# Sums of weights written over the raw chunk in a streaming fp32 encoder trunk

## The chip, the core and the metric

The kernel runs on one core of one Trainium2 chip. Its engines are named as in the profile: PE (TensorE, with PEld for its weight loads), DVE (VectorE), ACT (ScalarE), POOL (GpSimd) and SP (SyncE, which here only issues transfers). Each engine works through its own queue in order, and semaphores hold an instruction until what it needs is there. The metric is the time of one execution on the device, in microseconds; lower is better.

## What is computed

Two layers of an encoder over 256 positions of width 2048, all in float32. The first layer mixes positions with a gated MLP, the second with latent attention; each mixer is followed by a gated MLP with a short convolution:

```python
z = gelu(x @ w_in); u, v = split(z)             # 2048 -> 2 x 6144
s = einsum(w_s * mask, layer_norm(v)) + b_s
x = layer_norm(ALPHA * x + (u * s) @ w_out)     # 6144 -> 2048
h = causal_conv3(x @ w_up) + conv_b             # 2048 -> 2 x 5504
a, g = split(h)
x = layer_norm(ALPHA * x + (silu(g) * a) @ w_down)   # 5504 -> 2048
# second layer: low-rank q/kv projections, 16 heads, rotary part, masked softmax,
# output projection, then the same conv MLP
```

Weights are read once from memory (some 540 MB), so the kernel streams them in chunks of 1 MB.

## The kernel before

**Precision by splitting.** PE multiplies in a rounded fp32 form. Each operand is split into a rounded part and a remainder: ACT casts (`wh`, line 119 or 127), DVE subtracts (`wl`, line 120 or 128). A product is then three matmuls: high by high, low by high, high by low.

**Chunks and pairs.** `Feed` (line 72) loads chunks in a fixed order, splits them and hands them out. `next()` (line 197) hands out the next one and, before that, sees to it that a number of later chunks are split (`splits`) and loaded (`loads`). In the stages v (the second half of the first projection), wo (`w_out`) and dn (`w_down`) a chunk is a pair of 128-row blocks of weights against a pair of blocks of activations, 128x2048 values in four blocks of 512 columns. Such a pair is of one of three kinds:

- wide (`eight`, line 408): eight block products, 24 matmuls.
- seven (`seven`, line 415): Strassen's scheme in Winograd's form, seven block products, 21 matmuls. It needs four sums of the weight blocks (`_seven`, line 130) and of the activations. The sums of weights are made by DVE from the raw chunk (line 134), then split like the weights themselves into `th` and `tl`. The partial results are put together at the end of a group by `rest` (line 425): ACT copies one bank, DVE does four additions; these wait for the last seven products of the group.
- parked: a seven pair whose splitting is done long ahead, in the u and up stages, by `park` (line 146). The four parts go to memory through POOL's queue and are fetched again by `_fetch` (line 179) when the pair comes up for loading.

The v stage has six groups of eight pairs; group 0 is all wide, groups 1 to 5 hold four wide and four seven pairs each (order: wide, seven, wide, seven, wide, seven, seven, wide). wo goes twice over 24 pairs (7 seven pairs each time), each dn stage twice over 21 pairs and a half (10 seven and 8 parked in all). That makes 54 seven pairs and 16 parked ones. The other stages (u, up, the attention's projections, mo) have none.

**Buffers.** On-chip tiles of chunk size come from two sets: "big" with 17 places, "side" with 6. A place comes free when the last instruction that reads its tile is done, and whoever takes it next waits for that: a load waits on SP's queue, a fetch on POOL's. A seven pair takes `raw`, the sums `ts`, `wh`, `wl`, `th` and `tl`.

**What sets the order.** A scheduler places the instructions of each engine when the program is built, by priority and its own estimate of times. `behind` (line 227) adds ordering edges by which a transfer is placed not ahead of the matmul issued last in program order; it adds no wait. With them, the loads of the first chunks stand behind the nine warm-up matmuls (lines 269 and 270) in that order.

In `_seven`, DVE makes the sums into a tile of its own, in three operations (the first makes two sums at once), and the cast of the sums is made in two pieces:

```python
add(two(t, 0), two(raw, 512), raw[:, None, 0:512].to_broadcast([P, 2, 512]))
add(t[:, 1024:1536], t[:, 0:512], raw[:, 1024:1536])
self._cast(wh[:, 0:1536], wl[:, 0:1536], raw[:, 512:2048])
add(t[:, 1536:2048], t[:, 1024:1536], raw[:, 1536:2048])
for c in (slice(0, 1536), slice(1536, 2048)):
    self._cast(th[:, c], tl[:, c], t[:, c])
```

Of the kernel before, what the change touches and what calls it, by code (L numbers as in the profile page):

```python
# [8 lines left out]
F32 = mybir.dt.float32  # L9
F32R = mybir.dt.float32r  # L10
BF16 = mybir.dt.bfloat16
AF = mybir.ActivationFunctionType
ALU = mybir.AluOpType
AX = mybir.AxisListType

P = 128
# [44 lines left out]
        NF_FF: ("0e 1e 2s 3e 4p 5s 6e 7e 8s 9e 10e 11p 12s 13e 14e 15s 16e 17s 18p 19e 20e 21e",  # L61
                "21e 20p 19e 18p 17s 16e 15p 14s 13e 12e 11p 10s 9e 8e 7p 6s 5e 4e 3e 2e 1e 0e")}
KINDS = {"e": "wide", "s": "seven", "p": "parked"}
KEEP = {"wide": 5, "seven": 9, "parked": 6}


# [5 lines left out]
class Feed:  # L72
# [10 lines left out]
    def _load(self):  # L83
        ap, cols, kind = self.chunks[self.loaded][:3]
        if kind == "parked":
            self.parts[self.loaded] = self._fetch(self.loaded)
            self.loaded += 1
            return
        t = self.pool.tile([P, 2048], F32, tag="big", name=f"raw{self.loaded}", bufs=SLOTS["big"])
        step = 512 if self.loaded == 0 else cols  # L90
        if len(ap.shape) == 3:
            self.behind(self.nc.sync.dma_start(t.rearrange("p (k c) -> p k c", k=ap.shape[1]), ap))
        else:
            if self.loaded in (1, 2):
                step = 1024
            for o in range(0, cols, step):
                self.behind(self.nc.sync.dma_start(t[:, o : o + step], ap[:, o : o + step]))
                if self.loaded == 0 and o == step:
                    self.between[0]()
        self.raw[self.loaded] = t  # L100
        self.loaded += 1
# [28 lines left out]
    def _seven(self, i, raw):  # L130

        add = lambda o, a, b: self.nc.vector.tensor_tensor(o, a, b, ALU.add)  # L134
        tile = lambda name, dt: self.pool.tile([P, 2048], dt, tag="big", name=f"{name}{i}", bufs=SLOTS["big"])
        t, wh, wl, th, tl = tile("ts", F32), tile("wh", F32R), tile("wl", F32R), tile("th", F32R), tile("tl", F32R)
        two = lambda a, o: a[:, o : o + 1024].rearrange("p (n c) -> p n c", n=2)
        add(two(t, 0), two(raw, 512), raw[:, None, 0:512].to_broadcast([P, 2, 512]))
        add(t[:, 1024:1536], t[:, 0:512], raw[:, 1024:1536])
        self._cast(wh[:, 0:1536], wl[:, 0:1536], raw[:, 512:2048])  # L140
        add(t[:, 1536:2048], t[:, 1024:1536], raw[:, 1536:2048])
        for c in (slice(0, 1536), slice(1536, 2048)):
            self._cast(th[:, c], tl[:, c], t[:, c])
        return wh, wl, th, tl

    def park(self, i):

        nc, pin = self.nc, self.pin
        tile = lambda n, dt: self.pool.tile([P, 2048], dt, tag="side", name=f"{n}{i}", bufs=SLOTS["side"])
        add = lambda o, a, b: pin(nc.vector.tensor_tensor(o, a, b, ALU.add))  # L150
        two = lambda a, o: a[:, o : o + 1024].rearrange("p (n c) -> p n c", n=2)
        self.kept[i] = kept = {}

        def store(n, t, cols):
            d = self.dram.tile([P, cols], F32, tag=f"kept{n}{i}", name=f"kept{n}{i}", bufs=1)
            pin(nc.gpsimd.dma_start(d, t[:, 0:cols].bitcast(F32)))
            kept[n] = d

        ap = self.chunks[i][0]
        raw = tile("praw", F32)  # L160
        pin(nc.gpsimd.dma_start(raw.rearrange("p (k c) -> p k c", k=ap.shape[1]), ap))
        yield
        yield
        yield
        t = tile("pts", F32)
        add(two(t, 0), two(raw, 512), raw[:, None, 0:512].to_broadcast([P, 2, 512]))
        add(t[:, 1024:1536], t[:, 0:512], raw[:, 1024:1536])
        add(t[:, 1536:2048], t[:, 1024:1536], raw[:, 1536:2048])
        yield
        for n, src, o, cols in (("w", raw, 512, 1536), ("t", t, 0, 2048)):  # L170
            hi, lo = tile(f"p{n}h", F32R), tile(f"p{n}l", F32R)
            pin(nc.scalar.copy(hi[:, 0:cols], src[:, o : o + cols]))
            pin(nc.vector.tensor_tensor(lo[:, 0:cols], src[:, o : o + cols], hi[:, 0:cols].bitcast(F32), ALU.subtract))
            store(f"{n}h", hi, cols)
            store(f"{n}l", lo, cols)
            if n == "w":
                yield

    def _fetch(self, i):

        got = []
        for n in ("wh", "wl", "th", "tl"):
            d = self.kept[i].pop(n)
            t = self.pool.tile([P, 2048], F32R, tag="side", name=f"f{n}{i}", bufs=SLOTS["side"])
            self.behind(self.nc.gpsimd.dma_start(t[:, 0 : d.shape[1]], d))
            got.append(t)
        return got

    def ahead(self, n_load, n_split):
        while self.split < min(n_split, len(self.chunks)):  # L190
# [6 lines left out]
    def next(self, splits=2, loads=2):  # L197
        i = self.used
        self.ahead(i + 1 + splits + loads, i + 1 + splits)
        self.used += 1  # L200
        return self.parts.pop(i)


@with_exitstack
def trunk(ctx: ExitStack, tc: tile.TileContext, x, xT, gm_in, gm_wout, ffn_up, ffn_dn,
          ml_q, ml_kv, ml_b, ml_out, consts, w_sT, b_s, ropes, ln_rows, out):
    nc = tc.nc
# [8 lines left out]
    recent = [None]  # L216
# [9 lines left out]

    def behind(ins):

        if recent[0] is not None:
            tc.add_manual_dep(ins.ins, recent[0].ins.name, mybir.DependencyInfo(mybir.DependencyClass.NoSync,  # L230
                                                                       mybir.DependencyReason.DATA), reason="pace")


    chunks, parked = [], []
# [57 lines left out]
    for j in range(4):  # L292
        t = slot([P, 4, S], f"xraw{j}")
# [103 lines left out]
    class Banks:  # L397
# [17 lines left out]
        def seven(self, a, sums, wh, wl, th, tl):  # L415
            s1, s2, s3, s4 = sums
            self.to("q3", s4, wh, wl, 512)
            self.to("p2", a[0][1], wh, wl, 1024)
            self.to("p1", a[0][0], wh, wl, 0)
            self.to("q4", a[1][1], th, tl, 1536)  # L420
            self.to("q5", s1, th, tl, 0)
            self.to("p7", s3, th, tl, 512)
            self.to("p6", s2, th, tl, 1024)

        def rest(self):
# [150 lines left out]
    class Norm:  # L576
# [11 lines left out]
        def fetch(self, h):  # L588

            if h in self.res:  # L590
                return
            t = slot([P, 2, 1024], f"res{self.idx}_{h}")
            for b in range(2):
                src = x[b * P : (b + 1) * P, h * 1024 : (h + 1) * 1024] if self.away is None else self.away[h][:, b, :]
                nc.sync.dma_start(t[:, b, :], src)
            self.res[h] = t
# [98 lines left out]
    for gi in range(6):  # L695

        acc = Banks(f"v{gi}", DIRECT if gi == 0 else DIRECT + OWN if gi % 2 else OWN + DIRECT)
        rest = (None,) * 4
        for c, p in enumerate(V_PAIRS[gi]):
            a = [[x_parts(xhl, 2 * p + j, b) for j in range(2)] for b in range(2)]  # L700
            got = feed.next()
            if p in V_SEVEN[gi]:
                acc.seven(a, xc[p], *got)
                if p == V_SEVEN[gi][-1]:
                    rest = acc.rest()
            else:
                acc.eight(a, *got)
            if gi == 0 and p in V_SEVEN[1]:
                x4 = xraw[p // 2]
                room = xc_room[len(xc) // 2][:, len(xc) % 2, :]  # L710
                xc[p] = combine(p, room, x4[:, 2 * (p % 2)], x4[:, 2 * (p % 2) + 1])
            if c == 2 and gi > 0:
                stats(gi - 1)
        vt = slot([P, 2, 1024], f"v{gi}", tag="side")
        for i, (n, t) in enumerate(zip(DIRECT, rest)):
            o = vt[:, i // 2, (i % 2) * 512 : (i % 2) * 512 + 512]
            if t is not None:
                nc.vector.tensor_tensor(o, acc.acc[n], t, ALU.add)
            nc.scalar.activation(o, acc.acc[n] if t is None else o, AF.Gelu_apprx_tanh,
                                 accum_out=vsum[:, i // 2, 2 * gi + i % 2 : 2 * gi + i % 2 + 1])  # L720
        v.append(vt)
        if gi == 0:
            nc.sync.dma_start(cst, consts)
            nc.sync.dma_start(rope_sb, ropes)

            lnrow = tp.tile([P, P], F32, tag="t1", name="lnrow", bufs=T1)
            nc.sync.dma_start(lnrow, ln_rows.rearrange("r (k p) -> (r k) p", p=P))
        if gi == 4:

            wT = slot([P, 2, 1024], "wT")  # L730
            wTg = wT[:, 0, :].rearrange("p (g i) -> p g i", g=NG)
            nc.sync.dma_start(wTg, w_sT)
            nc.gpsimd.memset(wTg[64:P, :, 0:64], 0.0)
            bsum = slot([P, 2, 1024], "bsum")
            nc.sync.dma_start(bsum[:, 1, :], b_s.to_broadcast([P, 1024]))
# [517 lines left out]
```

## Time and profile before

| | |
|---|---|
| median of 3 runs | 2503.91 us (2501.18 to 2511.24) |
| the profiled execution | 2503.74 us, span 2501.9 us |
| busy share of the span: PE, PEld, DVE, ACT | 99%, 85%, 79%, 57% |
| memory read and written | 539 MB and 65 MB, 241 GB/s over the span |
| stages by time (us from the span's start) | v to about 262, u to 560, wo to 815, up to 1288, dn to 1520, attention and mo to 1860, second up to 2264, second dn to 2502 |

A row of busy time by stage gives the stretch and its length, then for PE, PEld, DVE, ACT and POOL the busy time with the number of instructions in brackets, then the granted clock of PE as a share of full speed, the busy share of the DMA engines and GB/s. A row of the timeline gives start, duration, engine, line, operation, output and inputs with their shapes, and in square brackets the engine's idle time just before and what ended it. A row of waits gives who waited for whom, the total in us, how often, and the longest. A row of the chain of waits gives start, length and the work; a row of groups the busy time, the mean of one in ns, and the idle time before. Matmuls overlap in the records: their rate is read from the starts.

### The profile page before, as it was taken

The page shows a single profiled execution, that of the slowest core. Times are in us where ns is not written, and L with a number is a line of the kernel's source. Part 1 is how long each engine was busy: PE and PEld are TensorE (multiplying, and loading weights), DVE is VectorE, ACT ScalarE, POOL GpSimd, SP SyncE. Part 2 cuts the span into 40 slices and gives each one's busy share as a digit, 9 for nine tenths or more (in the row PEclk, how much of TensorE's full clock was granted, in tenths as well). Part 3 has the DMA queues.
Part 4 walks back from the last instruction along what each step waited for, and adds up shares of the span by engine and source line. Part 5 has one row for each costly group of instructions (what it writes and reads, how often), then busy time and mean ns, then how long its engine had stood idle before and what let it go on. Part 6 is the DMA issues. An engine that isn't in the chain of part 4 may idle for free.

```text
span 2501.9 us, 33396 instructions
## 1 busy us (share of the span) xinstructions
PE 2472.1 (99%) x12995; PEld 2123.2 (85%) x12995; DVE 1987.7 (79%) x2779; ACT 1425.2 (57%) x1976; POOL 84.8 (3%) x165
## 2 busy tenths in 40 slices
PE   9999999999999999999999999999999999999998
PEld 7887888888888888888887878988888888887886
DVE  6999866679898798796678878856698787768887
ACT  5666644456565666565555456564566665555543
POOL 0000000000000010000000100000000000000010
PEclk9999999999999999999999999999999999999999
DMA  6555644556566689787547984543589789556795
GB/s 245 201 217 203 218 170 169 185 178 216 201 201 214 247 337 356 293 331 277 185 168 286 341 323 165 181 168 129 189 315 352 277 340 361 200 173 231 278 375 196
DMA packets 109503, 606.17 MB, mean 242 GB/s; under 512 B 10272, under 2 KB 11040, under 8 KB 62112
## 3 DMA queue, kind: packets, MB, share of 16 engines
q1 hardware_dynamic: 85984, 465.61, 52.0%
q0 software_dynamic: 23360, 138.42, 14.1%
q8 instruction: 102, 1.67, 0.2%
q14 instruction: 57, 0.47, 0.1%
HBM read 538.98 MB, written 65.01 MB: 241 GB/s over the span
## 4 chain that ended last, share of the span: by engine, by line
PE 87%; DVE 5%; DMA 4%; issue 2%; ACT 1%; SPq 0%; POOL 0%; DVEq 0%; ACTq 0%; POOLq 0%
PE up L225 35%; PE u L225 11%; PE wo_q L225 5%; PE v_q L225 4%; PE dn_q L225 4%; PE mo L225 4%; PE v_p L225 4%; PE wo_p L225 3%; PE dn_p L225 3%; DMA raw<-in_ffn_dn_dram 3%; PE wo_e L225 2%; PE upf L225 2%; PE v_e L225 1%; DVE wl L120 1%; PE dn_e L225 1%
## 5 line engine op out<-in xcount | busy, mean ns | idle before, releaser
L120 DVE TENSOR_TENSOR wl<-raw,wh 128x1024 fp32r<-128x1024 f32 (+3 forms) x640 | 877.9, 1392 | 241.4 <-ACT wh L119 211.4
L119 ACT CAST wh<-raw 128x1024 fp32r<-128x1024 f32 (+3 forms) x640 | 743.4, 1189 | 336.2 <-DVE wl L120 71.2
L225 PE MATMUL up<-xhl,wh 128*128 128x512 f32 x2624 | 611.1, 390 | 0.0
L225 PEld LDWEIGHTS up<-xhl,wh 128*128 128x128 f32 x2624 | 487.4, 188 | 97.7
L225 PEld LDWEIGHTS up<-xhl,wl 128*128 128x128 f32 x2624 | 325.8, 192 | 6.4
L225 PE MATMUL up<-xhl,wl 128*128 128x256 f32 x2624 | 328.1, 283 | 0.0
L225 PE MATMUL u<-xhl,wh 128*128 128x512 f32 x768 | 182.5, 392 | 0.2 <-DVE h_u L380 0.2
L225 PEld LDWEIGHTS u<-xhl,wh 128*128 128x128 f32 x768 | 141.7, 188 | 29.0 <-DVE h_u L380 0.7
L127 ACT CAST th<-ts 128x1536 fp32r<-128x1536 f32 x106 | 111.2, 1052 | 86.4 <-DVE ts L134 76.0
L128 DVE TENSOR_TENSOR tl<-ts,th 128x1536 fp32r<-128x1536 f32 x106 | 126.4, 1219 | 0.6 <-ACT th L127 0.2
L225 PEld LDWEIGHTS u<-xhl,wl 128*128 128x128 f32 x768 | 95.6, 191 | 3.1 <-DVE wl L120 1.0
L127 ACT CAST wh<-raw 128x1536 fp32r<-128x1536 f32 x53 | 78.5, 1481 | 33.6 <-DVE wl L120 8.3
L225 PE MATMUL u<-xhl,wl 128*128 128x256 f32 x768 | 96.6, 283 | 0.8 <-DVE wl L120 0.8
L128 DVE TENSOR_TENSOR wl<-raw,wh 128x1536 fp32r<-128x1536 f32 x53 | 92.9, 1752 | 0.5 <-PE wo_p L225 0.4
L225 PE MATMUL mo<-wh,oT 128*128 128x512 f32 x256 | 82.6, 403 | 0.0
L134 DVE TENSOR_TENSOR ts<-raw 128x1024 f32<-128x1024 f32 x53 | 64.7, 1220 | 17.4 <-DMA raw<-in_ffn_dn_dram 10.4
L225 PE MATMUL v_q<-wh,xhl 128*128 128x512 f32 x224 | 70.2, 395 | 4.6 <-ACT wh L119 4.6
L134 DVE TENSOR_TENSOR ts<-ts,raw 128x512 f32<-128x512 f32 x106 | 72.7, 686 | 0.8
L225 PE MATMUL v_p<-wh,xhl 128*128 128x512 f32 x192 | 61.0, 395 | 1.0 <-ACT wh L119 1.0
L225 PEld LDWEIGHTS v_q<-wh,xhl 128*128 128x128 f32 x224 | 42.4, 190 | 14.4 <-ACT wh L119 5.7
L378 ACT COPY lo_u<-u 128x256 f32<-128x256 f32 x48 | 17.4, 362 | 60.0 <-PE u L225 60.0
L225 PEld LDWEIGHTS mo<-wh,oT 128*128 128x128 f32 x256 | 45.4, 189 | 7.1
(1703 smaller groups left out, 4255.2 us busy)
## 6 DMA issues: line engine op xcount, KB each, us to landing
raw<-in_ffn_up_dram SPq DMA_DIRECT2D x172, 1024.0 KB, 6.6
raw<-in_gm_in_dram SPq DMA_DIRECT2D x93, 1024.0 KB, 4.7
raw<-in_ffn_dn_dram SPq DMA_DIRECT2D x68, 1024.0 KB, 7.9
raw<-in_gm_wout_dram SPq DMA_DIRECT2D x48, 1024.0 KB, 5.1
praw<-in_ffn_dn_dram POOLq DMA_DIRECT2D x16, 1024.0 KB, 15.3
keptth<-pth POOLq DMA_DIRECT2D x16, 1024.0 KB, 9.4
kepttl<-ptl POOLq DMA_DIRECT2D x16, 1024.0 KB, 11.6
fth<-keptth POOLq DMA_DIRECT2D x16, 1024.0 KB, 9.2
```

The lines of the kernel that those rows point to most:

```text
L119: self.nc.scalar.copy(hi[:, c], raw[:, c])
L120: self.nc.vector.tensor_tensor(lo[:, c], raw[:, c], hi[:, c].bitcast(F32), ALU.subtract)
L127: self.nc.scalar.copy(hi, raw)
L128: self.nc.vector.tensor_tensor(lo, raw, hi.bitcast(F32), ALU.subtract)
L134: add = lambda o, a, b: self.nc.vector.tensor_tensor(o, a, b, ALU.add)
L225: recent[0] = nc.tensor.matmul(o, l, r, start=start, stop=stop, skip_group_check=True)
L378: nc.scalar.copy(lo, acc[:, S : 2 * S])
```

## The change

Five edits:

1. In `_seven` the tile `ts` is gone. The four sums are written over the four blocks of the raw chunk, one DVE operation of 512 columns each, after the raw weights themselves have been cast and subtracted. The sums are then cast in one piece of 2048 columns. Two of the sums have changed places, and `seven` reads them there. `park` does the same.
2. Parked parts are fetched from `next()`, for the nearest parked pair within five pairs, instead of when the loading comes to them.
3. `behind` adds no edge as long as no chunk has been handed out.
4. In the v stage the last two pairs of a group ask for three chunks split and one more loaded, instead of two and two.
5. `fetch` does nothing for a chunk that is already fetched.

```diff
+LEAD = 5
     def _load(self):
         if kind == "parked":
-            self.parts[self.loaded] = self._fetch(self.loaded)
+            self.fetch(self.loaded)
...
     def _seven(self, i, raw):
-        t, wh, wl, th, tl = tile("ts", F32), tile("wh", F32R), tile("wl", F32R), tile("th", F32R), tile("tl", F32R)
-        two = lambda a, o: a[:, o : o + 1024].rearrange("p (n c) -> p n c", n=2)
-        add(two(t, 0), two(raw, 512), raw[:, None, 0:512].to_broadcast([P, 2, 512]))
-        add(t[:, 1024:1536], t[:, 0:512], raw[:, 1024:1536])
+        wh, wl = tile("wh", F32R), tile("wl", F32R)
         self._cast(wh[:, 0:1536], wl[:, 0:1536], raw[:, 512:2048])
-        add(t[:, 1536:2048], t[:, 1024:1536], raw[:, 1536:2048])
-        for c in (slice(0, 1536), slice(1536, 2048)):
-            self._cast(th[:, c], tl[:, c], t[:, c])
+        self._sums(raw, add)
+        th, tl = tile("th", F32R), tile("tl", F32R)
+        self._cast(th, tl, raw)
         return wh, wl, th, tl
+
+    def _sums(self, raw, add):
+        r = [raw[:, 512 * i : 512 * (i + 1)] for i in range(4)]
+        add(r[1], r[1], r[0])
+        add(r[0], r[0], r[2])
+        add(r[2], r[2], r[1])
+        add(r[3], r[3], r[2])
...
+    def fetch(self, i):
+        if i in self.parts:
+            return
+        got = self.parts[i] = []
...
     def next(self, splits=2, loads=2):
         i = self.used
         self.ahead(i + 1 + splits + loads, i + 1 + splits)
         self.used += 1
-        return self.parts.pop(i)
+        got = self.parts.pop(i)
+        near = [j for j in range(i + 1, min(i + 1 + LEAD, len(self.chunks))) if self.chunks[j][2] == "parked"]
+        if near and self.chunks[near[0]][2] == "parked" and near[0] in self.kept:
+            self.fetch(near[0])
+        return got
...
     def behind(ins):
-        if recent[0] is not None:
+        if recent[0] is not None and feed.used > 0:
...
-            self.to("q5", s1, th, tl, 0)
-            self.to("p7", s3, th, tl, 512)
+            self.to("q5", s1, th, tl, 512)
+            self.to("p7", s3, th, tl, 0)
...
-            got = feed.next()
+            got = feed.next(splits=3 if c > 5 else 2, loads=1 if c > 5 else 2)
```

More of the change, by code (lines that the diff above doesn't have):

```diff
@@ L150, in park @@
         add = lambda o, a, b: pin(nc.vector.tensor_tensor(o, a, b, ALU.add))
-        two = lambda a, o: a[:, o : o + 1024].rearrange("p (n c) -> p n c", n=2)
         self.kept[i] = kept = {}
@@ L164, in park @@
         yield
[L165 to L170, printed above, removed]
+        for n, o, cols in (("w", 512, 1536), ("t", 0, 2048)):
             hi, lo = tile(f"p{n}h", F32R), tile(f"p{n}l", F32R)
-            pin(nc.scalar.copy(hi[:, 0:cols], src[:, o : o + cols]))
-            pin(nc.vector.tensor_tensor(lo[:, 0:cols], src[:, o : o + cols], hi[:, 0:cols].bitcast(F32), ALU.subtract))
+            pin(nc.scalar.copy(hi[:, 0:cols], raw[:, o : o + cols]))
+            pin(nc.vector.tensor_tensor(lo[:, 0:cols], raw[:, o : o + cols], hi[:, 0:cols].bitcast(F32), ALU.subtract))
             store(f"{n}h", hi, cols)
@@ L177, in park @@
                 yield
-    def _fetch(self, i):
-        got = []
+                self._sums(raw, add)
+                yield
+    def fetch(self, i):
+        if i in self.parts:
+            return
+        got = self.parts[i] = []
         for n in ("wh", "wl", "th", "tl"):
@@ L186, in _fetch @@
             got.append(t)
-        return got
     def ahead(self, n_load, n_split):
```

## The prediction

> **What bounds the kernel now.** I read the page's busy shares first, then what TensorE (PE) waits for, then busy time by stage.
>
> ```profile
> span 2501.9 us, 33396 instructions
> PE 2472.1 (99%) x12995; PEld 2123.2 (85%) x12995; DVE 1987.7 (79%) x2779; ACT 1425.2 (57%) x1976; POOL 84.8 (3%) x165
> ```
>
> ```profile
> PE v_q L225 <- ACT wh L119: 4.6, 2, 3.3
> PE dn_q L225 <- DVE tl L128: 3.4, 2, 1.7
> PE dn_q L225 <- DVE dn03wx L467: 2.3, 1, 2.3
> ```
>
> ```profile
> 110.00:160.00 50.00, 50.00 (x222) 41.40 (x221) 47.97 (x43) 32.64 (x38) 0.00 (x0) 1.00 0.57 204
> 262.00:560.00 298.00, 296.95 (x1761) 263.40 (x1760) 207.54 (x377) 142.66 (x221) 0.84 (x1) 1.00 0.51 178
> 560.00:690.00 130.00, 130.00 (x575) 107.65 (x574) 118.57 (x137) 74.56 (x70) 0.00 (x0) 1.00 0.63 211
> 1288.00:1400.00 112.00, 108.03 (x473) 88.14 (x472) 99.69 (x130) 63.72 (x68) 6.36 (x12) 1.00 0.71 257
> 1400.00:1520.00 120.00, 117.20 (x515) 95.64 (x514) 96.08 (x121) 58.95 (x61) 8.74 (x18) 1.00 0.82 306
> ```
>
> PE is the bound nearly everywhere: 29.8 us of 2501.9 are idle, in waits of a few us. So little can be won. But VectorE (DVE) stands close behind in the stages that hold seven-product pairs: 47.97 us of 50 in the v stage (96%), 91% in wo (560 to 690), 89% and 80% in dn, against 70% in the u stage, which has none. A change to the seven pairs is therefore read from the v stage. The chain of waits shows its rhythm: each of the v groups 1 to 5 (four wide pairs of 24 matmuls, four seven pairs of 21) takes exactly 40.80 us, and 12 matmuls take 2.72 us, 0.227 us each; 180 x 0.227 is that 40.8.
>
> ```profile
> 95.57 2.72 PE v_q L225 x12
> 136.37 2.72 PE v_q L225 x12
> 177.17 2.72 PE v_q L225 x12
> ```
>
> How DVE spends such a group is seen in its timeline:
>
> ```profile
> 148.00 1.22 DVE L134 TENSOR_TENSOR ts<-raw 128x1024 f32<-128x1024 f32 x1
> 149.26 0.69 DVE L134 TENSOR_TENSOR ts<-ts,raw 128x512 f32<-128x512 f32 x1
> 149.87 1.75 DVE L128 TENSOR_TENSOR wl<-raw,wh 128x1536 fp32r<-128x1536 f32 x1
> 151.54 0.68 DVE L134 TENSOR_TENSOR ts<-ts,raw 128x512 f32<-128x512 f32 x1
> 152.14 1.75 DVE L128 TENSOR_TENSOR tl<-ts,th 128x1536 fp32r<-128x1536 f32 x1
> 153.81 2.28 DVE L120 TENSOR_TENSOR wl<-raw,wh 128x2048 fp32r<-128x2048 f32 x1
> 156.01 0.68 DVE L128 TENSOR_TENSOR tl<-ts,th 128x512 fp32r<-128x512 f32 x1
> 172.97 0.69 DVE L431 TENSOR_TENSOR v3u<-v_p,v3p 128x512 f32<-128x512 f32 x1 [1.27 <-PE v_p L225]
> 174.91 2.28 DVE L120 TENSOR_TENSOR wl<-raw,wh 128x2048 fp32r<-128x2048 f32 x1
> ```
>
> ```profile
> 149.98 1.49 ACT L127 CAST th<-ts 128x1536 fp32r<-128x1536 f32 x1 [0.42 <-DVE ts L134]
> L119 ACT CAST wh<-raw 128x2048 fp32r<-128x2048 f32 x19 | 36.3, 1910 | 1.4 <-PE v_p L225 0.8 <-PE v_q L225 0.6
> ```
>
> DVE runs without a gap because ScalarE (ACT) makes `th` from the first 1536 sums (149.98) while DVE subtracts `wl`: when DVE comes to `tl` at 152.14, `th` is there. A group holds 1.27 us of DVE idleness, the wait for PE before the fold. And the next group's first `wl` starts at 174.91, ready at 177.2, when PE wants it at 177.17: no lead to spend.
>
> **The change: seven pairs.** Two prices come from the timeline. An operation that needs nothing of its predecessor starts before that one's record ends (151.54 after 149.87: 1.67 for 1.75; 156.01 after 153.81: 2.20 for 2.28). One that needs its result starts 0.04 us after the end (149.26 after 148.00 + 1.22). A hop from DVE to ACT costs 0.03 (149.26 + 0.69 to 149.98). Today a seven pair takes 5.81 us (148.00 to 153.81) plus 0.60 for the last `tl`: 6.41 us.
>
> The changed program's queues put on DVE: `wl`, four sums, `tl`, and nothing else between sums and `tl` in 53 of the 54 seven pairs. Each sum depends on its predecessor, the first on `wl`, because they write over `raw`. ACT's one cast waits for the fourth sum, and `tl` for the whole cast. So: `wl` 1.75 + 0.04; three sums of 0.69 + 0.04; the fourth 0.69; hop 0.03; cast of 2048 on ACT 1.91; hop 0.03; `tl` 2.20. That is 8.84 us, 2.43 more. DVE's work hardly changes; 1.97 us are a pause in which DVE's queue stands behind `tl`, with the next pair's `wl` and the folds behind it. The cover that is lost is the `wl` subtraction that lay beside `th`. ACT loses nothing (57% busy).
>
> On the dependent start the Trainium skill (VectorE: DVE Perf Modes, "The DRAIN you can't avoid") says that a semaphore between chained vector operations costs nothing extra. The two starts above disagree, by 0.12 us. By the page the four dependent starts would cost 0.5 us less, some 8 us less over the 16 pairs of groups 2 to 5.
>
> A group is then, on DVE: four wide pairs at 2.20, eight fold operations at 0.61, four seven pairs at 8.84: 8.8 + 4.9 + 35.4 = 49.1; the pair whose sums alternate with fold operations saves 0.3, and one `wl` waits as long for ACT. 49.0 against 40.8, so 8.2 us more in each of groups 2 to 5: 32.8, less the 1.3 us that PE waits there already (4.6 less 3.3). The earlier split (`splits=3` for the last two pairs) gives no lead, since the fold that waits for PE still stands ahead of the next group's `wl`.
>
> Group 1 pays more, once:
>
> ```profile
> 54.78 0.60 ACT L719 ACTIVATE v<-v_p 128x512 f32<-128x512 f32 x1 [0.22 <-PE v_p L225]
> 61.74 2.29 DVE L120 TENSOR_TENSOR wl<-raw,wh 128x2048 fp32r<-128x2048 f32 x1
> L692 ACT ACTIVATE vsq<-v,vc 128x512 f32<-128x512 f32 x20 | 14.2, 712 | 0.0
> 90.13 1.36 PE v_p L225 x6
> ```
>
> ACT's new order is: two GELUs (the second at 54.78), `wh9`, two GELUs, `th9`, four squares with a small cast among them, then `wh10`. `wh9` ends at 56.9, `wl9` at 58.6, the sums at 61.6, `th9` at 63.6, `tl9` at 65.8; the small cast needs a DVE result from behind `tl9`, three squares follow, so `wh10` runs 68.8 to 70.7 and `wl10` starts at 70.7 instead of 61.74. From there 2.20 + 8.84 + 2.20 + 8.84 + 8.84 = 30.9 to 101.6, and PE's last eight matmuls of that pair end at 103.4 instead of 90.13: +13.3. The v stage: 13.3 + 32.8 - 1.3 = **+44.8 us**. The u stage behind it has 30% of DVE free but gives nothing back, as PE fills it.
>
> **wo and dn.** Three pairs (two wide, one seven) take PE 69 x 0.227 = 15.65 us; DVE works 15.65 x 118.57/130 = 14.3 of them. With 2.43 more it needs 16.7: 1.1 us short every three pairs. Here DVE has a lead:
>
> ```profile
> 601.88 2.35 DVE L128 TENSOR_TENSOR tl<-ts,th 128x1536 fp32r<-128x1536 f32 x2
> 610.72 2.04 PE wo_q L225 x9
> ```
>
> The `tl` of this pair is done at 604.2, and PE wants it after nine matmuls, at 612.8: 8.5 us, less the pause 6.1. Seven seven pairs in a half use up 7 x 1.1 = 7.7 us of it, so 1.6 reach PE in the first half; the run of six wide pairs at the turn restores the lead, and in the second half it is less: +2 us. If the lead is nothing, it is 14 x 1.1 = 15 us: the upper end. The two dn stages are alike (20 seven pairs), but parked pairs in between cost DVE little; the waits for `tl` there (3.4 us) stay or grow: +2 each, between -4 (the smaller set of buffers brings the late load sooner) and +10.
>
> **Parked parts.** Fetching five pairs ahead moves nothing: the first fetch of each pair already waits on POOL's queue for PE to free its buffer,
>
> ```profile
> POOL fwh L185 <- PE dn_p L225: 497.9, 10, 178.1
> ```
>
> and in the changed program the same fetches wait for the same matmuls; POOL's order differs in three places, no fetch among them. Parking itself: 16 sets of sums, each 4 x 0.73 = 2.9 us instead of 1.22 + 2 x 0.69 less overlaps, half a us more, behind spare DVE time in u and up: 0. The swapped `th` offsets: 0.
>
> **The start.** Without the ordering edges the first weights are issued second, ahead of constants and ropes:
>
> ```profile
> 0.74 1.81 SPq L296 DMA_DIRECT2D xraw<-in_xT_dram  x4
> 3.55 1.85 SPq L97 DMA_DIRECT2D raw<-in_gm_in_dram  x4
> 1.32 3.82 PE L225 MATMUL warm<-idle 128*128 128x512 bf16 x9 [1.32 <-POOL idle L267]
> 8.45 1.22 PE L225 MATMUL v_q<-wh,xhl 128*128 128x512 f32 x2 [3.32 <-ACT wh L119]
> 10.66 0.80 PE L225 MATMUL v_p<-wh,xhl 128*128 128x512 f32 x1 [0.99 <-ACT wh L119]
> ```
>
> One issue takes 0.47 us, so weights leave at 1.2 instead of 3.55: at least 2.35 us won; at most the whole 3.3 + 1.0 of PE's two waits and a clock that is up sooner, some 6. I take 4, nearest to the waits.
>
> **Sum.** The profiled execution took 2503.74 us, the median is 2503.91, so one base serves: 2503.7 - 4 + 44.8 + 2 + 4 = 2550.5, **2550 us**, 1.9% slower. A difference of 0.5% (12.5 us) is about what can be told from no change.
>
> **Rivals.**
> (a) Not slower: the pause is absorbed in the v stage, because buffers given up by the separate sums let DVE run ahead. The point that decides is a group's DVE time of 40.8 us: it would need 8.2 us more lead in every group. Then only the start counts: 2500. For it: one buffer fewer per seven pair. Against it: the fold stands ahead of the next `wl` in the queue. 0.06.
> (b) TensorE's clock drops in the new pauses. Cold, the nine warm-up matmuls take 3.82 us, some 0.425 apart. At that rate groups 2 to 5 take 180 x 0.425 = 76.5 us, 27.5 over 49: +110, so 2660. Against it: the longest new pause of PE is that of DVE's sums and the cast (2.9 + 1.97, less two us of products that PE still has), about 3 us, and the 2.3 us wait in 1400 to 1520 left the clock at 1.00. The Trainium skill (TensorE: Matmul & The Clock Gate, Part 1) has the clock halved after an idle window of about 3.4 us, which would put these pauses just below it. 0.05.
> (c) The change does what its words say on the parked side: fetches start sooner and collide with raw loads in dn, where transfers fill 0.71 to 0.82. Each stage's 4 us of waits might double twice over: +16, 2566. Against it: the unchanged waits of POOL. 0.04.
> (d) Half of the pause is hidden, in some pairs, by what I cannot see: 4 us a group and a cheaper group 1: 2503.7 - 4 + 16 + 8 + 4 = 2528. 0.08.
> The forecast has the rest, 0.77, by itself between 2534 (dependent starts no dearer than others, -8; no loss in wo and dn, -6; 6 won at the start, -2) and 2574 (wo without lead, +13; one dn stage at its end, +10).
>
> The range 2522 to 2580 takes in (c) and (d) and the bounds, and leaves out (a) and (b). Faster by over 0.5%: 0.04, if (a) comes with fewer waits in dn; within 0.5%: 0.05; slower by over 0.5%: 0.91.
>
> **What would show it.** Right: DVE waits `tl` <- ACT `th` of about 2 us, 54 times, over 100 us in all; PE in 110 to 160 us about 83% busy and waiting for `tl`, `th` and `wl`; group starts in the chain 49 us apart; first real matmul at 4 to 6 us; u, up and mo as long as before. Wrong: groups still 40.8 us apart, or PE's clock below 1.00 after the first 60 us.

## The result and the profile after

The changed kernel takes 2584.47 us (median; 2582.92 to 2584.87) against 2505.75 us before (2501.18 to 2511.24): a ratio of 1.031, 95% interval 1.029 to 1.0335. It is slower, as forecast, but by 79 us instead of 46, and the time lies just above the range. The profiled execution took 2584.63 us, with a span of 2582.9. The page of the kernel after begins with the span and the busy shares:

```profile
span 2582.9 us, 33370 instructions
PE 2509.0 (97%) x12995; PEld 2132.8 (83%) x12995; DVE 2008.2 (78%) x2795; ACT 1411.1 (55%) x1923; POOL 84.6 (3%) x165
```

TensorE (PE) has the same 12995 matmuls and is busy 37 us longer with them: some of them ran slower. VectorE's (DVE's) busy time has grown by only 20 us. Who waited for whom, for PE and then for DVE (total, times, longest):

```profile
PE v_q L232 <- ACT th L128: 20.6, 12, 3.8
PE dn_q L232 <- ACT th L128: 7.5, 6, 2.9
PE lnt L675 <- DVE res L662: 4.4, 2, 2.2
PE u L232 <- DVE wl L121: 3.8, 1, 3.8
...
PE v_q L232 <- ACT wh L120: 3.6, 1, 3.6
PE upf L232 <- ACT xhl L682: 2.0, 1, 2.0
PE mq L232 <- ACT xhl L682: 2.0, 1, 2.0
```

```profile
DVE tl L129 <- ACT th L128: 107.6, 52, 2.8
```

The last line is the forecast's "over 100 us": DVE's queue stands behind `tl` about 2 us for every pair. (There are 53 seven pairs, as both profiles count them, and not 54: the second half of wo has six.) One v group of the kernel after, in DVE's timeline:

```profile
137.08 2.29 DVE L129 TENSOR_TENSOR tl<-raw,th 128x2048 fp32r<-128x2048 f32 x1 [2.02 <-ACT th L128]
139.29 1.75 DVE L129 TENSOR_TENSOR wl<-raw,wh 128x1536 fp32r<-128x1536 f32 x1
141.08 2.87 DVE L135 TENSOR_TENSOR raw<-raw 128x512 f32<-128x512 f32 x4
145.97 2.29 DVE L129 TENSOR_TENSOR tl<-raw,th 128x2048 fp32r<-128x2048 f32 x1 [2.02 <-ACT th L128]
148.18 2.28 DVE L121 TENSOR_TENSOR wl<-raw,wh 128x2048 fp32r<-128x2048 f32 x1
151.71 0.69 DVE L438 TENSOR_TENSOR v2u<-v_p,v2p 128x512 f32<-128x512 f32 x1 [1.25 <-PE v_p L232]
...
165.77 2.29 DVE L129 TENSOR_TENSOR tl<-raw,th 128x2048 fp32r<-128x2048 f32 x1 [2.77 <-ACT th L128]
```

From `tl` at 137.08 to `tl` at 145.97 one seven pair takes 8.89 us (forecast: 8.84). The first fold of each group (line 438) starts as follows, by the view of that line (minimum, median and maximum duration in ns, first and last start):

```profile
L438 DVE TENSOR_TENSOR v2u<-v_p,v2p x1: 693/693/693, 151.7 to 151.7; 128x512 f32<-128x512 f32 x1
L438 DVE TENSOR_TENSOR v3u<-v_p,v3p x1: 692/692/692, 202.9 to 202.9; 128x512 f32<-128x512 f32 x1
```

So a group takes 51.2 us; before, the same two folds start at 132.4 and 173.0, 40.6 apart; the forecast had 49.0. What PE does in the same group (timeline), and the granted clock of the six microseconds behind its pause (the number 0.50, third from the end):

```profile
141.57 0.61 PE L232 MATMUL v_p<-wl,xhl 128*128 128x512 f32 x2
145.99 1.22 PE L232 MATMUL v_q<-th,xhl 128*128 128x512 f32 x2 [3.81 <-ACT th L128]
147.01 1.06 PE L232 MATMUL v_q<-th,xc 128*128 128x512 f32 x2
```

```profile
146.00:152.00 6.00, 6.00 (x14) 4.41 (x15) 4.75 (x3) 4.91 (x3) 0.00 (x0) 0.50 0.00 0
```

PE waits 3.81 us for `th` of the second of two seven pairs that follow each other, and then runs 14 matmuls in 6 us, 0.43 us each instead of 0.227. The starts of the same matmul in both traces, before and after, tell where the time went: first products (by matmul 100) -5.0 us; behind the first fold of group 1 +7.1, which is +12.1 for the group; first fold of group 1 to that of group 5 +40.2; from there to 20 us into u +2.8; wo +5.9; the turn from wo to the first up +6.5; first dn +3.7; the turn to the attention +6.2; second up +1.1; second dn and the norm behind it +7.5. Between those stages nothing moves: u, the first up, the attention and mo take as long as before. Together +81.0, the difference of the spans. The two turns look like this on PE (timeline of the kernel after):

```profile
862.19 0.39 PE L232 MATMUL wo_q<-wl,wo1wx 128*128 128x512 f32 x1
864.77 1.11 PE L675 MATMUL lnt<-ident,res 128*128 128x128 f32 x8 [2.20 <-DVE res L662]
867.89 0.79 PE L232 MATMUL upf<-wh,xhl 128*128 128x512 f32 x1 [2.00 <-ACT xhl L682]
```

Before, the transposes for the norm (`lnt`) lay among the last wo products, the first at 802.55:

```profile
802.32 0.39 PE L225 MATMUL wo_q<-wh,wo3wx 128*128 128x512 f32 x1
802.55 0.60 PE L668 MATMUL lnt<-ident,res 128*128 128x128 f32 x4
```

Of the 6.5 us of the turn behind wo, 4.2 are these two waits; the rest goes with the clock, which stands at 0.50 for 6.8 us from 865.8 on. The reason for the waits stands in DVE's queue, whose order was fixed when the program was built. First before, then after: where the statistics (`lnst`) followed each residual sum, two weight subtractions and the next sum now stand ahead of them.

```profile
795.48 0.68 DVE L640 TENSOR_TENSOR res<-res,wo_q 128x512 f32<-128x512 f32 x1
796.19 0.69 DVE L643 BATCH_NORM_STATS2 lnst<-res 128x6 f32<-128x512 f32 x1
```

```profile
856.04 0.69 DVE L647 TENSOR_TENSOR res<-res,wo_q 128x512 f32<-128x512 f32 x1 [1.39 <-PE wo_q L232]
857.17 0.69 DVE L647 TENSOR_TENSOR res<-res,wo_p 128x512 f32<-128x512 f32 x1 [0.45 <-PE wo_p L232]
857.78 2.35 DVE L121 TENSOR_TENSOR wl<-raw,wh 128x1024 fp32r<-128x1024 f32 x2
860.05 1.28 DVE L650 BATCH_NORM_STATS2 lnst<-res 128x6 f32<-128x512 f32 x2
```

### The profile page after: what moved, and what is told of

It reads as the page before. It is cut to its first block, busy times and chain, and to the rows that moved or that the text cites. A ratio compares the mean times of both kernels' runs of the same rounds, so it can differ in the third digit from the quotient of the medians.

```text
span 2582.9 us, 33370 instructions
## 1 busy us (share of the span) xinstructions
PE 2509.0 (97%) x12995; PEld 2132.8 (83%) x12995; DVE 2008.2 (78%) x2795; ACT 1411.1 (55%) x1923; POOL 84.6 (3%) x165
## 4 chain that ended last, share of the span: by engine, by line
PE 67%; DVE 13%; issue 9%; ACT 6%; DMA 4%; POOL 1%; SPq 0%; DVEq 0%; ACTq 0%; POOLq 0%
PE up L232 26%; PE u L232 10%; PE dn_q L232 5%; DVE wl L121 4%; PE dn_p L232 4%; PE mo L232 3%; DVE raw L135 3%; PE wo_q L232 2%; DMA praw<-in_ffn_dn_dram 2%; DVE wl L129 2%; PE v_q L232 2%; PE upf L232 2%; ACT th L128 2%; PE dn_e L232 2%; PE wo_p L232 2%
## 5 line engine op out<-in xcount | busy, mean ns | idle before, releaser
L128 ACT CAST th<-raw 128x2048 fp32r<-128x2048 f32 x53 | 101.0, 1906 | 218.9 <-DVE raw L135 207.2
L129 DVE TENSOR_TENSOR tl<-raw,th 128x2048 fp32r<-128x2048 f32 x53 | 121.5, 2293 | 109.7 <-ACT th L128 107.6
L135 DVE TENSOR_TENSOR raw<-raw 128x512 f32<-128x512 f32 x212 | 146.6, 691 | 6.2
L173 DVE TENSOR_TENSOR pwl<-praw,pwh 128x1536 fp32r<-128x1536 f32 x16 | 28.1, 1758 | 30.5 <-ACT pwh L172 30.5
```

Source lines behind the costliest of these rows:

```text
L128: self.nc.scalar.copy(hi, raw)
L129: self.nc.vector.tensor_tensor(lo, raw, hi.bitcast(F32), ALU.subtract)
L173: pin(nc.vector.tensor_tensor(lo[:, 0:cols], raw[:, o : o + cols], hi[:, 0:cols].bitcast(F32), ALU.subtract))
```

## The experiments

The theory: DVE's queue stands behind the one-piece cast of `th` with nothing beside it. Rivals: writing the sums over the raw chunk costs it (longer chains, sums that must stand behind `wl`); the fetches, the splits or the start have a part; PE's clock has a part of its own. Ratios are to the kernel before, with 95% intervals; "group" is the distance of the first folds of v groups 2 and 3.

| kernel | us | ratio | group, us |
|---|---|---|---|
| before | 2503.6 to 2505.8 | | 40.6 |
| after | 2584.5 | 1.031 [1.029, 1.0335] | 51.2 |
| all but the sums | 2505.4 | 1.0005 [0.9996, 1.0015] | 42.0 |
| the sums alone | 2581.2 | 1.030 [1.029, 1.032] | 51.2 |
| own tile, one piece | 2550.4 | 1.018 [1.0165, 1.020] | 49.6 |
| own tile, one piece, covered | 2509.5 | 1.0015 [1.0006, 1.0024] | 44.2 |
| over raw, pieces 1536 + 512 | 2533.5 | 1.011 [1.009, 1.013] | 46.3 |
| over raw, pieces of 1024 | 2528.3 | 1.009 [1.008, 1.011] | 47.7 |
| after, v as before | 2533.2 | 1.011 [1.010, 1.013] | 42.0 |
| after, late pairs as before | 2559.8 | 1.0215 [1.020, 1.023] | 51.2 |
| after, pause filled | 2576.2 | 1.029 [1.027, 1.030] | 49.5 |
| after, splits as before | 2575.4 | 1.0285 [1.027, 1.030] | 51.2 |
| the start alone | 2501.0 | 0.9986 [0.9977, 0.9995] | 40.6 |
| mix | 2490.6 | 0.9935 [0.992, 0.995] | 40.5 |

**Which part of the change: all but the sums.** `_seven`, `park` and the offsets in `seven` are those of before; what is left of the change:

```diff
-        if recent[0] is not None:
+        if recent[0] is not None and feed.used > 0:
...
-            got = feed.next()
+            got = feed.next(splits=3 if c > 5 else 2, loads=1 if c > 5 else 2)
...
+            self.fetch(near[0])
```

> All of the change but the sums: a tile of their own, th in two pieces, as before; the early start, the fetches five pairs ahead and the other splits in v stay changed. Theory (the one-piece cast is the whole loss): 2505.7 less 5 of the start, 2500.7 us, v groups 40.8 us apart, no new wait at the ends of wo and dn. Rival (the fetches or the other order of loads cost the 6.5 and 6.2 us at the ends of wo and of the first dn): 2513 us.

2505.4 us, and no waits at the ends of wo and dn: what after loses comes from the sums, and this rival falls. But the start was to win 5 us, and the total is no different from before. The trace shows the first products 5.6 us earlier and 3.6 us lost again in v groups 2 to 4, which take 42.0 us. Neither the start (its groups take 40.6 us, below) nor the fetches (the v stage has no parked pair) can do that: the earlier splits, costed at nothing, are not free.

**The sums alone**, on the kernel before (the same edit in `park`):

```diff
-        add(two(t, 0), two(raw, 512), raw[:, None, 0:512].to_broadcast([P, 2, 512]))
...
+        self._sums(raw, add)
+        th, tl = tile("th", F32R), tile("tl", F32R)
+        self._cast(th, tl, raw)
```

> The sums alone, written over the raw chunk and cast in one piece (parked pairs too); start, fetches and splits as before. Theory: after without its early start, 2584.5 + 5 = 2589 us, v groups 51 us apart, and the waits at the ends of wo and of the first dn are there. Rival (fetches or loads cause those waits): 2576 us without them.

2581.2 us, 8 below the expectation, with the waits at the two turns: they come from the sums. It is even 3.3 us faster than after, though it lacks the early start: the rest of the change costs something together with the sums, as the splits do (below).

**One piece or over the raw chunk?** All but the sums, with this edit:

```diff
         add(t[:, 1024:1536], t[:, 0:512], raw[:, 1024:1536])
+        add(t[:, 1536:2048], t[:, 1024:1536], raw[:, 1536:2048])
         self._cast(wh[:, 0:1536], wl[:, 0:1536], raw[:, 512:2048])
-        add(t[:, 1536:2048], t[:, 1024:1536], raw[:, 1536:2048])
-        for c in (slice(0, 1536), slice(1536, 2048)):
-            self._cast(th[:, c], tl[:, c], t[:, c])
+        self._cast(th, tl, t)
```

> As the kernel with all but the sums, but th is cast in one piece from the separate tile; the queue of VectorE still has the last sum straight ahead of tl. Theory (it is the uncovered cast, not the writing over the raw chunk): VectorE needs 8.40 us a pair (sums 1.26 + 0.61, wl 1.67, sum 0.69, hop 0.03, cast 1.91, hop 0.03, tl 2.20) against 8.89 in after, groups 51.2 - 4 x 0.49 = 49.2 us apart, total about 2584.5 - 5 x 2 - 3 = 2571 us. Rival (writing over the raw chunk costs it: longer chains and sums that must stand behind wl): about 2501 us.

The groups came out as expected (folds at 145.0 and 194.6, 49.6 apart; 49.3 in the next), so the rival falls as the whole cause: 45 us of the loss are there without a sum written over anything. But the other 34 us, from 2550.4 to 2584.5, appear only when the sums are also written over the raw chunk. The total is 20 us below the expectation, since only v and the turn behind wo lose (+37 us at the end of v, +8 at the turn); within wo it loses 1 us and in dn nothing, where after lost 5.9, 3.7 and about 4. That the own tile lets DVE run ahead there is argued, not shown. The waits of DVE in this kernel:

```profile
DVE tl L129 <- ACT th L128: 83.6, 50, 2.1
```

**The same with cover.** The last sum is held ahead of `wl` in DVE's queue by an order written out; nothing else differs in the source:

```diff
+        self.pin(self.nc.vector.tensor_tensor(t[:, 1536:2048], t[:, 1024:1536], raw[:, 1536:2048], ALU.add))
+        self.nc.scalar.copy(wh[:, 0:1536], raw[:, 512:2048])
+        self.pin(self.nc.vector.tensor_tensor(wl[:, 0:1536], raw[:, 512:2048], wh[:, 0:1536].bitcast(F32), ALU.subtract))
+        self._cast(th, tl, t)
```

> As the kernel with a tile of its own and th in one piece (2550.4 us), but all sums stand ahead of the weight's subtraction in VectorE's queue, so that the 1.91 us cast of th has the 1.75 us of wl beside it. Theory (it is the cover that counts, not the one piece): VectorE needs 6.7 us a pair instead of 8.4, pause 0.2 to 0.3 us; total that of the kernel with all but the sums plus 4 x 1.3: 2505.4 + 6 = 2511 us. Rival (one piece costs by itself, because TensorE's first th product and ScalarE's queue wait for the whole): above 2535 us.

2509.5 us. Moving one 0.69 us sum past one subtraction gives 41 us back with the cast still whole. DVE's timeline shows how little of the wait is left once `wl` lies beside the cast:

```profile
155.12 0.69 DVE L141 TENSOR_TENSOR ts<-ts,raw 128x512 f32<-128x512 f32 x1
155.73 1.75 DVE L143 TENSOR_TENSOR wl<-raw,wh 128x1536 fp32r<-128x1536 f32 x1
157.80 2.30 DVE L129 TENSOR_TENSOR tl<-ts,th 128x2048 fp32r<-128x2048 f32 x1 [0.32 <-ACT th L128]
```

**Over the raw chunk, in two pieces.** After, with the cast of `th` placed ahead of the last sums; once with 1024 columns (two sums are enough), once with 1536 (three):

```diff
-        self._sums(raw, add)
-        self._cast(th, tl, raw)
+        for i, (o, s, k) in enumerate(((1, 1, 0), (0, 0, 2), (2, 2, 1), (3, 3, 2))):
+            add(r[o], r[s], r[k])
+            if i == 1:
+                self.nc.scalar.copy(th[:, 0:1024], raw[:, 0:1024])
+        self.nc.vector.tensor_tensor(tl[:, 0:1024], raw[:, 0:1024], th[:, 0:1024].bitcast(F32), ALU.subtract)
+        self._cast(th[:, 1024:2048], tl[:, 1024:2048], raw[:, 1024:2048])
```

> After, with th and tl in two pieces of 1024 columns; the first piece of th is cast as soon as two sums are there, beside the other two. Sums still over the raw chunk. Theory: no pause; VectorE needs 1.79 + 3 x 0.73 + 0.61 + 2 x 1.15 = 6.9 us a pair instead of 8.89, groups 51.2 - 4 x 2.0 = 43.2 us apart, total about 2500.7 + 5 x 2.4 + 5 in wo and dn = 2518 us. Rival (writing over the raw chunk costs it): above 2565 us.

> After, with th and tl in two pieces of 1536 and 512 columns; the first piece of th is cast when three sums are there. Sums over the raw chunk. Half of the pause is left: th comes 0.03 + 1.49 + 0.03 us behind the third sum, of which the fourth covers 0.73, so tl waits 0.8 us instead of 2.0. Theory (the length of the pause is what is paid): VectorE needs 7.76 us a pair, between 8.89 (after, 2584.5 us) and 6.9 (pieces of 1024, 2528.3 us): 2584.5 - 56 x 1.13/1.99 = 2553 us. Rival (any pause behind tl costs the whole, since the queue stands): above 2570 us.

2528.3 and 2533.5 us: the rivals fall, and both sizes were missed, the first by 10 us upwards, the second by 20 downwards. With 1024 columns `tl` waits only 5.2 us in the whole program, but the group takes 47.7 us, not 43.2: at the turn of the group the built order puts the weight casts behind GELUs and squares on ScalarE (ACT), and DVE waits there instead (and 1.08 us for PE ahead of the fold):

```profile
158.94 2.29 DVE L121 TENSOR_TENSOR wl<-raw,wh 128x2048 fp32r<-128x2048 f32 x1 [2.62 <-ACT wh L120]
162.35 1.76 DVE L129 TENSOR_TENSOR wl<-raw,wh 128x1536 fp32r<-128x1536 f32 x1 [1.11 <-ACT wh L128]
```

With 1536 columns `tl` waits 50.0 us in all, 52 times, half as long as in after, and the group takes 46.3. Interpolating between two kernels with different orders was the mistake: a sum over this kernel's own queue, as in the prediction (four pairs of 7.76, four of 2.20, eight folds of 0.61), gives 44.7, and 45.3 with the wait of 0.96 that was measured for 0.82. This kernel lost 7.1 us at the turn behind wo, the one with 1024 0.1, so its total is the higher one.

**The clock.** After, with zeros multiplied in the pause; they are added into an open bank and change no value:

```diff
             self.to("p1", a[0][0], wh, wl, 0)
+            for _ in range(fill):          # 24 in the second last pair of v groups 1 to 5, else 0
+                mm(self.acc["q4"][:, 0:256], zero[:, 0:P], zero, False, False)
             self.to("q4", a[1][1], th, tl, 1536)
```

> After, with 24 matmuls of 256 columns with weights and data of zero added into an open bank in each of v groups 1 to 5, ahead of the products that wait 3.8 us for th; their sum is zero and the result unchanged. Theory (the lower clock behind that pause is a loss of its own): the pause is then under 1.5 us of idle TensorE, the clock stays at 1.00 and the fold comes 1.25 us sooner: groups 50.0 us apart instead of 51.2, total 2584.5 - 6 = 2578.5 us. Rival (VectorE alone sets the group, the clock costs nothing): groups 51.2 us apart, 2584.5 us.

2576.2 us, 8.3 less than after, with more work on PE. The same place in its timeline, and the clock of six microseconds behind it:

```profile
139.75 2.79 PE L232 MATMUL v_q<-zero 128*128 128x256 bf16 x24
143.71 0.73 PE L232 MATMUL v_q<-th,xhl 128*128 128x512 f32 x2 [1.17 <-ACT th L128]
```

```profile
144.00:150.00 6.00, 6.00 (x27) 4.74 (x27) 5.97 (x5) 4.67 (x3) 0.00 (x0) 1.00 0.16 26
```

27 matmuls run in 6 us instead of 14. The folds stand 49.5 us apart, and DVE no longer waits 1.25 us for PE ahead of the fold:

```profile
L442 DVE TENSOR_TENSOR v2u<-v_p,v2p x1: 681/681/681, 148.1 to 148.1; 128x512 f32<-128x512 f32 x1
L442 DVE TENSOR_TENSOR v3u<-v_p,v3p x1: 685/685/685, 197.6 to 197.6; 128x512 f32<-128x512 f32 x1
```

So a slow PE holds up the engine that holds up PE: 1.25 of the 1.7 us that a group is shorter are this wait. Rival (b) of the prediction was there, with 8 us instead of 110: it took the lower clock for whole groups, and it lasts 6.8 us of 51.2. The zeros cover one pause of a group only; in this kernel a wait of 2.40 us in group 3, ahead of 162.1 us, is still followed by a clock of 0.72 over six microseconds.

**The splits.** After, with those of the v stage as before:

```diff
-            got = feed.next(splits=3 if c > 5 else 2, loads=1 if c > 5 else 2)
+            got = feed.next()
```

> After, with the splits of the v stage as before (two ahead everywhere). Theory (three ahead puts a cast of raw weights behind GELUs and squares on ScalarE, or delays it, and costs the difference between after and the sums alone, 5.5 us in v and 4.3 us where u takes over): 2584.5 - 9.8 = 2574.7 us. Rival (the splits cost nothing, as forecast, and the 3 us between the two kernels are something else): 2584.5 us.

2575.4 us, as expected. Group 1 is 4.8 us shorter (its first fold at 95.8 instead of 100.5), groups 2 to 5 are as in after, and where u takes over PE waits half as long:

```profile
PE u L232 <- DVE wl L121: 1.9, 1, 1.9
```

**The stages.** After, with the v stage's sums made as before:

```diff
+        if i < 48:
+            return self._seven_v(i, raw)      # _seven of before
```

> After, but the v stage makes its sums as before (a tile of their own, th in two pieces); wo and both dn stages keep the change. Theory (each stage pays for its own pauses, the waits at the ends of wo and of the first dn among them): the v stage as in the kernel with all but the sums, 2.1 us below before there, then the +26 us that the trace of after shows behind v: 2503.6 - 2.1 + 26 = 2527 us. Rival (the waits at the ends of wo and dn are carried on from a v stage that ends late): they vanish, 2514 us.

2533.2 us, 6 above the expectation, which had 26 us behind v where the trace of after has 30.9 (5.9 + 6.5 + 3.7 + 6.2 + 1.1 + 7.5); here it is 32.4. Each stage pays for itself: the waits at the turns stay (+7.0 us behind wo) with a v stage that ends early. The next kernel asks which pairs of a stage make the turn late. After, with some sums as before in the later parts of wo and dn:

```diff
+                old = (True,) if kind == "seven" and hf == 1 and u in (0, 1, 2, 3, 4, 5, 6, 7, 8, 9, 10, 11, 12, 13, 14) else ()
```

> After, with the sums as before (own tile, two pieces) in the second halves of wo and of both dn stages; first halves and v as in after. In the built order the statistics of the norm behind wo then stand behind each residual sum again instead of behind two weight subtractions. Theory (the pauses of a second half make VectorE late at its end, and the order made for that lateness costs the 6.5 us behind wo and the 6.2 us behind the first dn): these vanish, and about 7 us of waits in the halves: 2584.5 - 12.7 - 7 = 2565 us. Rival (the losses at the ends have another cause): 2577 us.

As run, this changes ten pairs: the last four of the six in wo's second half and the last three of four in that of each dn. 2559.8 us, 5 below the expectation. Both turns are back to nearly nothing (+0.5 and 0.1 us across them), and in DVE's queue the statistics stand behind their residual sums again. So the sums of a stage's last pairs go with the order that costs the turn. That the scheduler chooses this order because its own estimate has DVE late at the end of a stage is argued, not shown.

**The start alone**, one line on the kernel before:

```diff
-        if recent[0] is not None:
+        if recent[0] is not None and feed.used > 0:
```

> Before, with only the ordering edges ahead of the first product left out. Theory: first real matmul at 4.8 us instead of 8.5, 4.8 us less at matmul 400 and nothing given back: 2503.6 - 4.8 = 2498.8 us. Rival (the gain is given back by waits in v, as in the kernel with all but the sums): 2502 to 2504 us.

2501.0 us, between the two: 3.3 us won at the first products and kept to the end of up; in the trace the waits of dn take half of it back. The row of the first products shows 4.78 instead of 8.45 us, and a wait of 1.47 behind them that was 0.99. From 9.0 to 12.4 us the clock of this execution stands at 0.50, where that of the mix below stays at 1.00 and wins 5.0 us:

```profile
4.78 1.19 PE L225 MATMUL v_q<-wh,xhl 128*128 128x512 f32 x2
7.43 0.50 PE L225 MATMUL v_p<-wh,xhl 128*128 128x512 f32 x1 [1.47 <-ACT wh L119]
```

**A mix of what paid:** the early start, fetches five ahead, v as before, and in wo and dn the sums over the raw chunk with `th` in pieces of 1024.

> The early start, fetches five pairs ahead, v stage as before (own tile, two pieces, two splits ahead), and in wo and dn the sums over the raw chunk with th in pieces of 1024. Theory (each part as measured alone: start -3.2, v 0, the two dn stages -3.6 and -3.0 as in the kernel with pieces of 1024 throughout): 2504.1 - 9.8 = 2494 us, faster than both. Rival (dn gained there only because TensorE came later to work that was ready): 2501 us.

2490.6 us, a ratio of 0.9935 [0.992, 0.995]: faster than both. Start -5.0, v and wo 0, first dn with its turn -6.4, second -2.8 with the norm behind it. It puts the three edits above together (`_seven_v` in v, pieces of 1024 elsewhere, `feed.next()`). PE's largest wait that is left:

```profile
PE dn_q L255 <- DMA ftl<-kepttl: 2.4, 2, 1.5
```

The waits of dn for `tl` are gone. All but the sums, which has the same fetches, won only 0.9 us in the first dn, so most of it belongs to the sums over the raw chunk; whether through the place that each pair gives up or through the order, no run separates.

## Where the prediction was right, and which steps failed

- **The mechanism** (DVE's queue stands behind `tl`, the cover of `wl` is lost) was right: 8.89 us a pair for 8.84, 107.6 us of waits. The kernel with the cover put back shows that it is this and not the one piece as such. By itself the uncovered cast costs 45 us; the other 34 need the sums over the raw chunk besides. The dependent sums cost what the two starts of before said: four in 2.87 us, 0.73 apart. The Trainium skill (VectorE: DVE Perf Modes, "The DRAIN you can't avoid") has a semaphore between chained operations at no cost; by the rows of independent ones, 0.60 apart, it would have been 2.5 us. The trace decides.
- **A group, 49.0 us**, was 51.2. Two items were left out: the fold's wait for PE, which the prediction had quoted (1.27 before, 1.25 after) and dropped from the sum, and `tl` behind ACT's GELUs and squares (2.77 instead of 2.0). The first survives only because PE is slow there: with the pause filled it goes.
- **The longest new pause of PE is "about 3 us", so no clock loss.** This step failed: it was 3.81 us. The prediction left PE two microseconds of products; at `wl`'s end (141.04) only 1.1 us of them were left (to 142.2), since the six with `wh` had run already. The clock then stood at 0.50 for 6 us, which the filled kernel prices at 8.3 us. The prediction's own sign of being wrong, a clock below 1.00 behind the first 60 us, is in the trace: 0.93 from 110 to 160 us. Nor would 3 us have been safe: in dn of the kernel after, a wait of 2.92 us (to 1448.6) was followed by a clock of 0.72 over six microseconds.
- **Group 1, +13.3**, was +12.1 and for the reason given, ACT's order; without the earlier splits it would have been 4.8 less.
- **"The earlier split gives no lead"**, costed at nothing: it costs 9.1 us with the sums, and about 4 without them. It is an edit of the order on ACT, and its cover was not named.
- **wo +2, dn +2 each** were +5.9, +3.7 and about +4, within the bounds given.
- **Turns between stages had no term at all.** They cost 6.5 and 6.2 us, and some 3 at the end. The prediction looked for lateness at `th` and `tl` and not at what else stands in DVE's queue when a stage ends. This is the second step that failed: a term put at nothing without a reason.
- **The start, -4**: -5.0 by matmul 100 in after, -3.3 alone. **Fetches and parking, 0**: right within 3 us (all but the sums behind v: -1.0); u and up have not moved, but for 1.1 us in the second up.
- **Sum.** The starts of the same matmuls, set against the terms of the prediction, give the whole miss of 34 us: start and group 1 together 2.2 us less than forecast; groups 2 to 5 and the turn into u +43.0 for +31.5, so 11.5 more; wo and the turn behind it +12.4 for +2, 10.4 more; all that follows +18.5 for +4, 14.5 more. The prices that the runs gave are not further items: 4.8 of the 9.1 us of the splits lie in group 1, whose term held them already, and part of the cost of each turn is the clock again.
- **The upper bound.** The 2574 counted 10 us for a dn stage at its end, though 2 of them were in the forecast already; and none of its items was the clock or a turn.

## What to carry to other kernels

When an operation is made whole or moved, ask what lay beside it: a 1.9 us cast with a 1.75 us subtraction next to it costs 0.3 us, and without it 2.0 us in every pair, since the queue behind it stands too. On a kernel with two engines near the bound, price the turns between stages and the clock behind each pause of PE as terms of their own, and measure "free" neighbours of the main edit (here the splits) by themselves. A part that loses in one stage may win in another: the sums over the raw chunk, in two pieces, are worth keeping in dn, cost nothing in wo, and do not pay in v.

## What was unexpected of the hardware

The clock does not fall at one length of pause. Pauses of 3.8 us were followed by a clock of one half each time. Pauses of 2.05 us in the kernel with pieces of 1536 + 512 were followed by different clocks in two groups with the same work. PE's timeline and the six microseconds behind each:

```profile
136.03 1.13 PE L237 MATMUL v_q<-th,xc 128*128 128x512 f32 x2 [2.05 <-ACT th L144]
...
182.32 0.73 PE L237 MATMUL v_q<-th,xc 128*128 128x512 f32 x2 [2.05 <-ACT th L144]
```

```profile
136.00:142.00 6.00, 5.97 (x19) 4.78 (x20) 5.96 (x6) 5.48 (x4) 0.00 (x0) 0.72 0.14 25
182.00:188.00 6.00, 5.68 (x24) 4.52 (x25) 5.66 (x5) 5.79 (x5) 0.00 (x0) 1.00 0.09 22
```

0.72 behind one, 1.00 behind the other. What differs is where the pause lies. In the trace's record of the granted clock, all changes stand whole multiples of 3.41 us apart, in this kernel (58.03 us is 17 times 3.41, 68.27 us is 20 times) and in each of the others. Cut along these boundaries, the same two places read:

```profile
132.80:136.20 3.40, 1.35 (x7) 0.81 (x6) 2.09 (x4) 2.18 (x3) 0.00 (x0) 0.99 0.92 342
136.20:139.60 3.40, 3.40 (x9) 2.62 (x10) 3.40 (x3) 3.40 (x3) 0.00 (x0) 0.50 0.01 2
180.60:184.00 3.40, 1.68 (x7) 1.42 (x8) 2.18 (x3) 3.40 (x4) 0.00 (x0) 1.00 0.45 190
184.00:187.40 3.40, 3.40 (x16) 2.61 (x16) 3.40 (x4) 3.40 (x3) 0.00 (x0) 1.00 0.00 0
```

The first pause lies whole in one stretch, in which PE is busy for 1.35 of 3.40 us, and the next stretch runs at half the clock. The second pause is cut by a boundary: PE is busy for 1.68 us, and the clock stays. Over the fourteen traces of this case, a stretch at full clock in which PE idled for 58% or more was followed by one at half in 57 of 57 cases, and one with 25 to 52% in 1 of 110; in between both occur (the ends of matmuls are modelled, so the shares are not exact). The Trainium skill (TensorE: Matmul & The Clock Gate, Part 1) has the clock halved after an idle window of about 3.4 us, and says that this window runs freely. The traces agree with the length and with the free running, but the window need not be idle throughout: a little over half of it is enough here. As an estimate from these shares (0.55 of 3.41 us), a pause of 1.9 us can cost the clock if it falls into one stretch, and one of 3.8 us costs it wherever it falls. For a forecast it means that a pause of 2 us is not safe.
